# A decoder trunk on one core: more gate and up pairs by seven products, the queries' row earlier, and an end by halves of the tokens

## The chip, the cores and the metric

The kernel runs on one core of a Trainium2 chip. Its engines work from queues of their own and wait for one another by semaphores: TensorE (PE, matmuls into PSUM), VectorE (DVE), ScalarE (ACT), GpSimd (POOL) and SyncE (SP, here only for DMA). The metric is the device time of one execution in microseconds (us), as the median of several runs. A profile is one execution, recorded instruction by instruction.

## The reference

Input x is (1, 512, 1024) in float32; width D is 1024, the feed-forward width 2816, there are 16 heads of 64 and two layers. Layer 0 mixes tokens by a convolution, layer 1 by stick-breaking attention against keys and values that are projected once between the layers:

```python
h = x
for layer in range(2):
    h = h + 0.5 * swiglu_ffn(rms_norm(h, ffn1_norm[layer]), ...)
    u = rms_norm(h, mix_norm[layer])
    if layer < 1:
        h = h + conformer_conv(u, ...)
    else:
        q = split_heads(u @ attn_w_q[0])
        o = stick_breaking_attention(q, k_shared, v_shared)
        h = h + o.transpose(0, 2, 1, 3).reshape(b, s, d) @ attn_w_o[0]
    h = h + 0.5 * swiglu_ffn(rms_norm(h, ffn2_norm[layer]), ...)
    if layer == 0:
        k_shared, v_shared = ...   # rms_norm(h, kv_norm) @ w_kv, in heads
return rms_norm(h, final_norm)

def swiglu_ffn(x, w_gate, w_up, w_down):
    return (silu(x @ w_gate) * (x @ w_up)) @ w_down
```

There are four feed-forward blocks. They are called stages 0 to 3 here, as the kernel numbers them.

## The kernel before

Everything is kept transposed: a tile has 128 channels as partitions and the 512 tokens as columns, and the residual stream `res` is eight such tiles. Every float32 operand of a matmul is split into a high and a low part (`hi` by a cast on ACT, `lo` by a subtraction on DVE, function `split`), and `mm3` makes three matmuls of each product: hi·hi, hi·lo, lo·hi. Weights arrive as units of 128 × 1024 by DMA on SP into `raw` (three buffers) and are split into `whi` and `wlo` (three buffers each). `unit()` takes the oldest unit and fetches another one ahead, in the order that `weight_order` lists. All tiles come from pools: a tile with a tag and `bufs=n` takes the place of the n-th tile before it and waits until that one is no longer read.

A feed-forward block (`ffn`) goes through 22 tiles f of the hidden width in thirds of 8, 8 and 6. For each f, a pair of products gives gate and up (`pg`); then SiLU, a product and a split give `hhi`, `hlo`. After each third come the eight down products (`pd`), each added to `res`. The norm's factor for each token (`rb`, the row `r`) is multiplied in behind the products; `Norm.factor` makes it: squares are summed over chunks (`acc`), over channels by matmuls with a column (`token_sums`, `ss`), then a root in small steps on DVE (`inv_root`), diagonal tiles (`dg`) of the roots' two parts, and matmuls with ones which spread these over all partitions (`spread`, `pb`).

A pair can be made in a second way, listed in the table `SEVEN` by stage. Gate and up weights and two chunks of x are seen as 2 × 2 blocks, and a scheme of seven products takes the place of eight, on quarters: a weight tile of 128 columns against half of the tokens (256). `sevens` prepares the left-hand sums (`st`, split into `sh`, `sl`; `uh`, `ul`), `right_sums` the right-hand ones, once in a stage behind each of the pairs 0 to 3 (`ts`, split into `thi`, `tlo`). `seven` makes 7 products of 4 × 3 matmuls, 84 of 256 columns, where the direct way has 48 of 512. In the profile the direct ones stand under L389 to L391 (`pg<-`), the quarters under L551 to L553.

In attention, `project_values` and `project_keys` (which also makes the queries `pq`) fill PE between the heads' work; `PROJECTIONS` says which projection stands behind which pair of heads. Their outputs share two PSUM banks (`pj`). `project_keys` calls `n_mix.factor` once, in its first run, and keeps the row in `rq`; each `pq` is multiplied by it into `qt`.

The program is written in order, and a scheduler with a cost model of its own then orders each engine's instructions; `tc.manual_schedule` keeps the written order. The convolution has a planner, which the change does not touch. At the end, the last norm's row is made behind the last down product, and eight results are written out, six by DVE and two by ACT and POOL.

## Time and profile before

| | us |
|---|---|
| median of 3 runs | 1923.2 (1921.57 to 1923.63) |
| profiled execution, its own time | 1922.7 |
| its span, from the first to the last instruction | 1920.9 |
| mean granted clock of PE | 0.995 of full |

The span is what the trace covers; 1.8 us lie around it. By the trace, stage 0 goes from the start to about 343 us, the convolution to about 559, stage 1 to about 884, stage 2 to about 1265, attention to about 1549 and stage 3 to 1904; the rest is the last norm and the output. Rows of the trace show start (us), duration (us), engine, line, operation, output and inputs by the program's names without their numbers, partitions and sizes, and in brackets the engine's idle time before it with what ended it. Matmuls overlap in the pipeline: their durations are longer than the spacing of their starts.

### The profile page before, as it was taken

What the parts mean: (1) busy time and instruction counts of PE and PEld (TensorE: products, weight loads), DVE (VectorE), ACT (ScalarE), POOL (GpSimd) and SP (SyncE); (2) the same over time, 40 slices, a digit from 0 to 9 for tenths busy, and PEclk for the clock granted to TensorE, in tenths of its full rate; (3) what the DMA queues carried; (4) which work ended last, traced back from release to release, by engine and by line L of the source; (5) the groups of instructions that cost most, each with busy time, mean ns of one, the idle gap of its engine ahead of it and who ended that gap; (6) DMA issues with size and microseconds to landing.
All of it is one profiled execution on the core that took longest, in us unless ns stands there. A gap on an engine that the chain in (4) does not pass through costs nothing.

```text
span 1920.9 us, 25824 instructions
## 1 busy us (share of the span) xinstructions
PE 1892.0 (98%) x9996; PEld 1621.6 (84%) x9996; DVE 1281.6 (67%) x2054; ACT 862.5 (45%) x1347; POOL 276.3 (14%) x261
## 2 busy tenths in 40 slices
PE   9999999999999999999999999999999999999997
PEld 7888888878998889898888988888888788888895
DVE  6544534598868567466875756768999768466575
ACT  5424323686544234244332433546778544233332
POOL 0302202089600000000000000004543100000000
PEclk9999999999999999999999999999999999999998
DMA  5756746444422333233333333442232223323322
GB/s 201 254 180 239 267 145 229 155 162 151 138 88 88 110 95 103 90 96 112 121 110 109 100 99 92 127 150 77 84 88 89 65 89 99 95 92 99 110 85 69
DMA packets 72522, 237.79 MB, mean 124 GB/s; under 512 B 8272, under 2 KB 8400, under 8 KB 72400
## 3 DMA queue, kind: packets, MB, share of 16 engines
q1 hardware_dynamic: 64624, 209.40, 34.2%
q10 hardware_dynamic: 7776, 26.74, 3.7%
q8 instruction: 78, 1.28, 0.3%
q14 instruction: 44, 0.36, 0.1%
HBM read 200.46 MB, written 31.46 MB: 121 GB/s over the span
## 4 chain that ended last, share of the span: by engine, by line
PE 93%; DVE 3%; ACT 2%; POOL 1%; DMA 1%; issue 1%; DVEq 0%; POOLq 0%; ACTq 0%
PE pg L389 11%; PE pg L391 11%; PE pg L390 11%; PE pd L389 8%; PE pd L390 8%; PE pd L391 8%; PE pg L553 5%; PE pg L552 5%; PE pg L551 5%; PE z L1187 2%; PE pa L389 1%; PE pa L391 1%; PE pa L390 1%; POOL ws L869 1%; PE po L389 1%; PE pv L389 1%
## 5 line engine op out<-in xcount | busy, mean ns | idle before, releaser
L244 ACT CAST whi<-raw 128x1024 fp32r<-128x1024 f32 (+2 forms) x306 | 312.1, 1026 | 612.9 <-PE pd L390 232.1
L245 DVE TENSOR_TENSOR wlo<-raw,whi 128x1024 fp32r<-128x1024 f32 (+2 forms) x306 | 371.2, 1217 | 48.7 <-ACT whi L244 48.6
L389 PE MATMUL pg<-xhi_f,whi 128*128 128x512 f32 x976 | 379.7, 391 | 1.3 <-ACT whi L244 1.2
L391 PE MATMUL pg<-xhi_f,wlo 128*128 128x512 f32 x976 | 380.3, 390 | 0.5 <-DVE wlo L245 0.5
L390 PE MATMUL pg<-xlo_f,whi 128*128 128x512 f32 x976 | 380.4, 390 | 0.0
L390 PE MATMUL pd<-hlo,whi 128*128 128x512 f32 x704 | 274.0, 389 | 0.0
L389 PE MATMUL pd<-hhi,whi 128*128 128x512 f32 x704 | 273.0, 391 | 0.5 <-ACT whi L244 0.4
L391 PE MATMUL pd<-hhi,wlo 128*128 128x512 f32 x704 | 271.7, 389 | 0.0
L389 PEld LDWEIGHTS pg<-xhi_f,whi 128*128 128x128 f32 x976 | 183.5, 188 | 39.7 <-ACT whi L244 1.6
L391 PEld LDWEIGHTS pg<-xhi_f,wlo 128*128 128x128 f32 x976 | 183.3, 188 | 38.6 <-DVE wlo L245 1.3
L390 PEld LDWEIGHTS pg<-xlo_f,whi 128*128 128x128 f32 x976 | 183.5, 188 | 36.5
L627 DVE SCALAR_TENSOR_TENSOR xpar<-pd,xpar 128x512 f32<-128x512 f32 x96 | 65.3, 689 | 166.4 <-PE pd L391 166.4
L389 PEld LDWEIGHTS pd<-hhi,whi 128*128 128x128 f32 x704 | 132.2, 188 | 31.5 <-ACT whi L244 5.2
L391 PEld LDWEIGHTS pd<-hhi,wlo 128*128 128x128 f32 x704 | 132.2, 188 | 27.5 <-DVE wlo L245 0.3
L390 PEld LDWEIGHTS pd<-hlo,whi 128*128 128x128 f32 x704 | 132.2, 188 | 26.3
L607 DVE TENSOR_TENSOR tu<-pg,r_f 128x512 f32<-128x512 f32 x61 | 42.1, 690 | 95.6 <-PE pg L391 95.3
L1086 POOL TENSOR_SCALAR_AFFINE_SELECT tri<-ones 128x128 f32<-128x128 f32 x1 | 0.3, 294 | 714.4 <-DVE tu L582 714.4
L869 POOL TENSOR_TENSOR ws<-ws,pr 128x256 f32<-128x256 f32 (+1 forms) x90 | 90.7, 1019 | 58.2 <-ACT pr L867 54.6
L245 POOL TENSOR_TENSOR plo<-praw,phi 128x1024 fp32r<-128x1024 f32 x24 | 58.1, 2422 | 275.9 <-ACT phi L244 269.7
L605 DVE TENSOR_TENSOR tg<-pg,r_f 128x512 f32<-128x512 f32 x61 | 42.0, 690 | 82.6 <-PE pg L391 82.6
L244 ACT CAST hhi<-tu 128x512 fp32r<-128x512 f32 x88 | 54.7, 623 | 91.4 <-DVE tu L582 55.7
L880 DVE SCALAR_TENSOR_TENSOR pc<-gl,xpar,pc 128x512 f32<-128x512 f32 (+1 forms) x145 | 88.4, 647 | 4.1 <-PE pc L859 2.3
(341 smaller groups left out, 3907.2 us busy)
## 6 DMA issues: line engine op xcount, KB each, us to landing
raw<-in_gu_dram SPq DMA_DIRECT2D x174, 512.0 KB, 3.6
raw<-in_dna_dram SPq DMA_DIRECT2D x64, 512.0 KB, 3.6
praw<-in_pw_dram SPq DMA_DIRECT2D x24, 512.0 KB, 4.2
aparth<-phi ACTq DMA_DIRECT2D x24, 512.0 KB, 2.6
apartl<-plo ACTq DMA_DIRECT2D x24, 512.0 KB, 3.9
raw<-in_dnb_dram SPq DMA_DIRECT2D x32, 384.0 KB, 3.1
whi<-aparth SPq DMA_DIRECT2D x21, 512.0 KB, 3.3
wlo<-apartl SPq DMA_DIRECT2D x21, 512.0 KB, 4.2
```

What stands on the lines that cost most here:

```text
L244: ins = A.copy(dst_hi, src)
L245: (G if on_pool else V).tensor_sub(dst_lo, src, dst_hi.bitcast(F32))
L389: PE.matmul(ps, w[0], x[0], start=first, stop=False)
L390: PE.matmul(ps, w[0], x[1], start=False, stop=False)
L391: PE.matmul(ps, w[1], x[0], start=False, stop=last)
L551: PE.matmul(d, a[0], b[0], start=first and q == 0, stop=False, skip_group_check=True)
L552: PE.matmul(d, a[0], b[1], start=False, stop=False, skip_group_check=True)
L553: PE.matmul(d, a[1], b[0], start=False, stop=last_, skip_group_check=True)
L607: V.tensor_mul(tu, pt[1], rb)
L627: V.scalar_tensor_tensor(res[d], pd, 0.5, res[d], op0=ALU.mult, op1=ALU.add)
L869: add("G", 1.28 * f + 0.1 * half, lambda pr=pr: G.tensor_add(accp, accp, pr()[:, at0]), r=[pr], w=[at_], rank=rank)
L880: add("V", 0.66 * f + 0.06 * half, lambda x=x, q=q: V.scalar_tensor_tensor(pc(), x(), q, pc(), op0=ALU.mult, op1=ALU.add), r=[gl], w=[pc], ...
```

## The change

There are four edits.

1. `SEVEN` lists 11, 10 and 11 pairs in stages 1, 2 and 3, where it listed 9 in each. Some follow directly on one another, and the last pair of each third is a direct one.
2. For room, two buffers become single: `st` (with `ts`), and the parts of a seven-product pair's second weight unit, which leave the three buffers of `whi` and `wlo` for one of their own.
3. The queries' row is made at attention's head, ahead of all projections.
4. The last three down products of stage 3 and the last norm go by halves of the tokens, in an order written by hand (`tail`). The first half's row is made beside the second half's products. DVE reads one PSUM copy of the row, ACT another. The list of `parts` in `Norm`, used at the end alone, goes.

```diff
-SEVEN = {1: (5, 7, 9, 11, 13, 15, 17, 19, 21), 2: (5, 7, 9, 11, 13, 15, 17, 19, 21), 3: (5, 7, 9, 11, 13, 15, 17, 19, 21)}
+STS = 1
+SEVEN = {1: (5, 6, 8, 9, 11, 12, 14, 16, 17, 19, 20), 2: (6, 8, 10, 11, 13, 14, 16, 17, 19, 20), 3: (5, 6, 8, 9, 11, 12, 14, 16, 17, 19, 20)}
...
         hi, lo = (
-            [wp.tile([P, UNIT], F32R, name=f"{n}{i}_{o}", tag=n, bufs=3) for o in range(2)]
+            [wp.tile([P, UNIT], F32R, name=f"{n}{i}_0", tag=n, bufs=3),
+             p.tile([P, UNIT], F32R, name=f"{n}{i}_1", tag=n, bufs=1)]
             for n in ("whi", "wlo")
         )
...
-        st = p.tile([P, UNIT], F32, name=f"st{i}", tag="st", bufs=2)
+        st = p.tile([P, UNIT], F32, name=f"st{i}", tag="st", bufs=STS)
...
-                t = hp.tile([P, 2 * T], F32, name=f"ts{idx}_{q}", tag="st", bufs=2)
+                t = hp.tile([P, 2 * T], F32, name=f"ts{idx}_{q}", tag="st", bufs=STS)
...
-                for d in range(NC):
+                for d in range(NC - TAIL if tail is not None and third == 2 else NC):
...
-            rq = []
+            rq = n_mix.factor(ps, ("z", "z"), bufs=Z_BANKS)
+            V.tensor_scalar_mul(rq, rq, HD ** -0.5)
...
-                if not rq:
-                    rq.append(n_mix.factor(ps, ("z", "z"), bufs=Z_BANKS))
-                    V.tensor_scalar_mul(rq[0], rq[0], HD ** -0.5)
...
+        a, b, e = ds                      # down products 5, 6, 7; second argument: half of the tokens
+        with tc.manual_schedule(engines={nc.tensor.engine, nc.vector.engine, nc.scalar.engine, nc.gpsimd.engine}):
+            product(a, 0)
+            leave(a, 0)                   # add to res on DVE, square on ACT
+            add(a, 0)                     # add to acc on DVE
...
+            product(e, 0)
+            leave(e, 0)
+            product(a, 1)
+            sums(0)                       # token sums on PE
+            product(b, 1)
+            leave(a, 1)
+            for d in (3, 4, 5):
+                gain(d, 0)                # ACT's part of a result
+            root(0)                       # DVE
+            product(e, 1)
+            leave(b, 1)
+            diagonal_rows(0)              # one half each on DVE and ACT
+            row(0)                        # PE, two copies
+            add(a, 1)
+            leave(e, 1)
+            add(b, 1)
+            sums(1)
+            rows(0)                       # copy of the row on ACT
+            for d in (6, 7):
+                gain(d, 0)
+            for d in (0, 3, 1, 4, 2, 5, 6, 7):
+                scale(d, 0)               # POOL for those with a gain, else DVE; DMA out
+            for d in (5, 6, 7):
+                gain(d, 1)
+            root(1)
+            diagonal_rows(1)
+            row(1)
+            rows(1)
+            for d in (0, 5, 1, 2, 6, 3, 4, 7):
+                scale(d, 1)
```

What the scheduler makes of it is seen at three places. First PE in stage 1, within the pairs 5 and 6, which are the first two seven-product pairs in a row; a name like `pg1_6_0` is stage, pair and accumulator. Before, behind four products of pair 5, direct matmuls of pair 6 follow:

```order
L552 MATMUL pg1_5_0_5600<-xlo_f2_0_7_4902,whi99_0_5427 128x256
L553 MATMUL pg1_5_0_5600<-xhi_f2_0_7_4901,wlo99_0_5429 128x256
L389 MATMUL pg1_6_0_5707<-xhi_f2_0_1_4889,whi100_5504 128x512
L390 MATMUL pg1_6_0_5707<-xlo_f2_0_1_4890,whi100_5504 128x512
L391 MATMUL pg1_6_0_5707<-xhi_f2_0_1_4889,wlo100_5505 128x512
L389 MATMUL pg1_6_0_5707<-xhi_f2_0_2_4894,whi100_5504 128x512
L390 MATMUL pg1_6_0_5707<-xlo_f2_0_2_4895,whi100_5504 128x512
L551 MATMUL pg1_5_1_5601<-thi1_0_1_5209,whi99_1_5428 128x256
```

Now pair 6 is in quarters, and behind its first ones stand direct matmuls of pair 7:

```order
L553 MATMUL pg1_5_1_5601<-thi1_3_1_5495,wlo99_1_5430 128x256
L551 MATMUL pg1_6_1_5716<-thi1_0_0_5207,sh100_5517 128x256
L552 MATMUL pg1_6_1_5716<-tlo1_0_0_5208,sh100_5517 128x256
L551 MATMUL pg1_6_2_5717<-thi1_0_0_5207,sh100_5517 128x256
L552 MATMUL pg1_6_2_5717<-tlo1_0_0_5208,sh100_5517 128x256
L393 MATMUL pg1_7_0_5822<-xhi_f2_0_1_4889,whi101_5553 128x512
L394 MATMUL pg1_7_0_5822<-xlo_f2_0_1_4890,whi101_5553 128x512
L395 MATMUL pg1_7_0_5822<-xhi_f2_0_1_4889,wlo101_5554 128x512
```

So between a pair's quarters and those of the next, work of a third pair has been moved in. Second, ACT at attention's head (`vs` are values, `ks` keys, `r_mix` is the queries' row). Before, the row's copy stands behind the casts of three weight units and the first keys:

```order
L1125 CAST vs1_11269<-pv0_3_11357 128x2x64
L244 CAST whi212_11387<-raw212_11386 128x1024
L1138 CAST ks0_0_11417<-pk0_11392 64x512
L1138 CAST ks0_1_11418<-pk0_11392 64x512
L244 CAST whi213_11427<-raw213_11426 128x1024
L244 CAST whi214_11691<-raw214_11690 128x1024
L414 COPY r_mix_1_11477<-pb_mix_1_11481 128x512
L1138 CAST ks1_0_11721<-pk1_11696 64x512
```

Now it stands between the last two copies of values:

```order
L247 CAST whi207_11482<-raw207_11481 128x1024
L247 CAST whi208_11488<-raw208_11487 128x1024
L1129 CAST vs0_11493<-pv0_3_11582 128x2x64
L418 COPY r_mix_1_11461<-pb_mix_1_11465 128x512
L1129 CAST vs1_11494<-pv0_3_11582 128x2x64
L247 CAST whi209_11612<-raw209_11611 128x1024
L1142 CAST ks0_0_11642<-pk0_11617 64x512
```

Its place has moved ahead of the first keys. Third, ACT's queue at the end. Before:

```order
L469 ACTIVATE sq_out_7_17265<-xpar_69 128x512
L1287 ACTIVATE out7_17324<-xpar_69 128x512
L1282 COPY rs_17315<-pb_out_17302 128x512
L1291 DMA out_0_dram<-out0_17321 128x512
L1291 DMA out_0_dram<-out6_17317 128x512
L1291 DMA out_0_dram<-out2_17331 128x512
L1291 DMA out_0_dram<-out4_17337 128x512
```

Now, from the copy of the first half's row on (`out6` and `out4` wait for POOL):

```order
L1360 COPY rs_out0_17696<-pb_out0a_17683 128x256
L1345 ACTIVATE out6_17698<-xpar_69 128x256
L1345 ACTIVATE out7_17700<-xpar_69 128x256
L1356 DMA out_0_dram<-out0_17702 128x256
L1356 DMA out_0_dram<-out4_17630 128x256
L1356 DMA out_0_dram<-out2_17712 128x256
L1356 DMA out_0_dram<-out6_17698 128x256
L1345 ACTIVATE out5_17632<-xpar_69 128x256
L1345 ACTIVATE out6_17698<-xpar_69 128x256
L1345 ACTIVATE out7_17700<-xpar_69 128x256
L1332 ACTIVATE dg_out1_0_17742<-ident_76,dp_out1_17739 128x128
L1332 ACTIVATE dg_out1_1_17745<-ident_76,dp_out1_17739 128x128
```

The diagonals of the second half's row, which the results of that half need, stand behind four DMAs and three gains.

More of the change, by code (lines that the diff above doesn't have):

```diff
@@ L64 @@
 PR_BUFS = 3
+TAIL = 3
 WARM = 10
@@ L422, in token_sums, with inv_root @@
                           start=i + b == 0, stop=i == len(src) - 1, skip_group_check=True)
-    def inv_root(y, v, name):
-        t = tp.tile([P, v.shape[-1]], F32, name=f"rt_{name}", tag="rt", bufs=1)
+    def inv_root(y, v, name, p=None):
+        t = (p or tp).tile([P, v.shape[-1]], F32, name=f"rt_{name}", tag="rt", bufs=1)
         V.tensor_scalar(y.bitcast(I32), v.bitcast(I32), 1, None, op0=ALU.logical_shift_right)
@@ L438, in decoder_kernel, with __init__ @@
     class Norm:
-        def __init__(self, name, gain, pool=None, apart=False):
+        def __init__(self, name, gain, pool=None):
             self.name, self.gain, self.pool = name, gain, pool or xp
@@ L446, in __init__ @@
             self.n = 0
-            self.parts, self.apart = [self.acc], apart
             self.order = []
@@ L469, in square @@
                 A.activation(sq, res[c], AF.Square)
-                if self.apart and self.n == NC - 1:
-                    self.parts.append(sq)
-                else:
-                    V.tensor_add(self.acc, self.acc, sq)
+                V.tensor_add(self.acc, self.acc, sq)
             self.n += 1
@@ L477, in factor @@
             ss = ps.tile([P, 4], F32, name=f"ss_{self.name}", tag=tags[0], bufs=bufs)
-            token_sums(ss, *self.parts)
+            token_sums(ss, self.acc)
             small = tp.tile([P, 4], F32, name=f"rs_{self.name}", tag="rs", bufs=1)
@@ L484, in factor, with ffn @@
             return spread(ps, small, self.name, r, tag=tags[1], bufs=bufs)
-    def ffn(idx, norm, done, early=None, beside=None, sums=None, late=None):
+    def ffn(idx, norm, done, early=None, beside=None, sums=None, late=None, tail=None):
         with ExitStack() as c:
@@ L634, in ffn @@
                             beside(pp_)
+            if tail is not None:
+                tail(c, ps, hid, hp)
     with ExitStack() as c:
@@ L763, in decoder_kernel @@
         add("-", 5.0, lambda: None, w=["acc"])
-        add("PE", 0.7, lambda: token_sums(ssm(), *n_mix.parts), r=["acc"], w=[ssm], rank=-2)
+        add("PE", 0.7, lambda: token_sums(ssm(), n_mix.acc), r=["acc"], w=[ssm], rank=-2)
         add("V", 8.0, mix_diagonals, r=[ssm], w=["dgm"], rank=-2)
@@ L1295, in _lay @@
+    ffn(3, n_f2, n_out.chunk, tail=tail)
 def _lay(a):
```

86 lines of the change are left out of this document (70 added, 16 removed).

## The prediction

> **What bounds the kernel now.** I read the page first: busy shares, the chain that ended last, the waits of PE. Then time in windows, and single instructions where PE waits or changes shape.
>
> ```profile
> span 1920.9 us, 25824 instructions
> PE 1892.0 (98%) x9996; PEld 1621.6 (84%) x9996; DVE 1281.6 (67%) x2054; ACT 862.5 (45%) x1347; POOL 276.3 (14%) x261
> PE 93%; DVE 3%; ACT 2%; POOL 1%; DMA 1%; issue 1%; DVEq 0%; POOLq 0%; ACTq 0%
> ```
>
> TensorE (PE) is busy for 1892.0 of 1920.9 us and carries 93% of the chain that ended last. A change shortens the program if it takes time from PE's stream, or from the few places where PE stands still:
>
> ```profile
> PE pq L389 <- DVE qt L1149: 3.1, 1, 3.1
> PE pg L391 <- DVE wlo L245: 0.5, 1, 0.5
> PE pg L553 <- DVE sl L245: 0.4, 1, 0.4
> ...
> 1276.00:1312.00 36.00, 32.86 (x146) 26.47 (x145) 18.72 (x32) 15.88 (x27) 0.53 (x2) 0.95 0.41 117
> 1312.00:1400.00 88.00, 88.00 (x531) 77.14 (x530) 83.64 (x139) 64.92 (x125) 46.80 (x47) 1.00 0.25 70
> 1480.00:1515.00 35.00, 29.02 (x146) 21.63 (x146) 28.78 (x52) 27.17 (x54) 7.21 (x7) 0.96 0.08 23
> 1297.00:1300.00 3.00, 3.00 (x8) 2.31 (x8) 2.36 (x4) 1.56 (x3) 0.00 (x0) 0.55 0.80 251
> ```
>
> The waits are: line, releaser, total us, times, longest. The windows show stretch, its length, then busy us of PE, weight loads, VectorE (DVE), ScalarE (ACT), GpSimd (POOL), and PE's granted clock. PE lacks about 3 us at attention's head (1276 to 1312) and 6 us at attention's end (1480 to 1515); the program's last 17 us are taken up under D. Between, it is full, and so in attention is DVE: 83.64 of 88 us.
>
> **A: five more pairs by seven products.** A table makes 32 of the 66 pairs of stages 1 to 3 by seven products, where 27 were. Matmuls overlap, so their cost is the spacing of starts:
>
> ```profile
> 589.65 0.39 PE L391 MATMUL pg<-xhi_f,wlo 128*128 128x512 f32 x1
> ...
> 608.01 0.39 PE L391 MATMUL pg<-xhi_f,wlo 128*128 128x512 f32 x1
> 608.24 0.28 PE L551 MATMUL pg<-xhi_f,whi 128*128 128x256 f32 x1
> ...
> 613.87 0.28 PE L553 MATMUL pg<-xhi_f,wlo 128*128 128x256 f32 x1
> ```
>
> From 589.65 to 608.01 there are 81 spacings of 512 columns: 0.2267 us each. From 608.24 to 613.87 there are 47 of 256: 0.1198. A direct pair has 48 of the first, 10.88 us; a seven-product pair 84 of the second, 10.06. The difference of 0.82, five times, is −4.1 us. Nothing hides this, because PE is the bound. The Trainium skill (TensorE: Matmul & The Clock Gate, Back-to-back issue gap) gives a warm spacing of N/2.4 + 2.5 ns, so 215.8 and 109.2 ns. By that the five pairs would save 5.9 us; the trace's spacings are 11 ns longer in both shapes, and the trace decides.
>
> **B: what the pairs in a row may cost.** A seven-product pair loads DVE more:
>
> ```profile
> 615.78 1.22 DVE L245 TENSOR_TENSOR wlo<-raw,whi 128x1024 fp32r<-128x1024 f32 x1
> 616.92 0.68 DVE L337 TENSOR_TENSOR raw<-raw,raw 128x512 f32<-128x512 f32 x1
> 617.52 0.68 DVE L338 TENSOR_TENSOR st<-st,raw 128x512 f32<-128x512 f32 x1
> 618.12 0.42 DVE L562 TENSOR_TENSOR v<-pg,m 128x256 f32<-128x256 f32 x1
> 618.45 0.42 DVE L564 TENSOR_TENSOR tg<-pg,v 128x256 f32<-128x256 f32 x1
> ```
>
> Starts here are 1.14 us apart behind a 1024-wide operation, 0.60 behind 512, 0.33 behind 256. A seven-product pair has on DVE three of 1024 (two `wlo`, `sl`), eight of 512 (four sums, `ul`, two multiplies and `hlo` on the way out) and seven of 256: 3.42 + 4.80 + 2.31 = 10.5 us, against PE's 10.06. A direct pair has 2 × 1.14 + 4 × 0.60 = 4.7 against 10.88. Two in a row and a direct one make 25.7 us for DVE and 31.0 for PE, so DVE keeps up if it can work ahead. Within a row it falls back by 2 × 0.45 = 0.9 us at most if nothing was prepared before. There are 14 such rows (5, 4 and 5 by stage), so the bounds are 0 and +12.6 us.
>
> Two buffers shrink to one as well: the sums (`st`, also the right-hand sums), and the second operand's parts (`whi`, `wlo` of `o` = 1). At the first row (pairs 5 and 6 of stage 1) I followed the queues with these spacings. The last right-hand sums now wait for pair 5's `sl`. They come near 611.1, and PE, which in the new order does 41 quarter matmuls before it reads them, needs them at 608.24 + 41 × 0.12 = 613.2. Pair 6's `sl` comes near 618.5, while PE has 21 direct matmuls of pair 7 in front of it, until about 623. Pair 6's `whi` and `wlo` of `o` = 1 need some 4 us after pair 5's last product, and PE has 28 quarter and 15 direct matmuls, 6.8 us, ahead of them. So margins are 2 to 5 us. The nearest measured row is the pair of short waits above: 0.5 and 0.4 us in all 27 seven-product pairs. I take +1.0 us for the changed rows. That no third ends in seven products I cost at nothing: PE has the down products' matmuls on the earlier `hid` tiles as cover, and without it a pair's way into `hid` (three to four DVE steps of 0.6) would stand open at most 2 us in nine places, as it could before.
>
> **C: the queries' row.** What held PE at attention's head:
>
> ```profile
> 1287.79 0.88 DVE L410 TENSOR_SCALAR dg_mix<-ident,dp_mix 128x128 fp32r<-128x128 f32 x4 [1.45 <-PE pb_mix L411]
> 1293.33 1.05 ACT L244 CAST whi<-raw 128x1024 fp32r<-128x1024 f32 x1 [4.91 <-PE pk L390]
> 1294.40 0.59 ACT L414 COPY r_mix<-pb_mix 128x512 f32<-128x512 f32 x1
> 1296.01 0.69 DVE L1149 TENSOR_TENSOR qt<-pq,r_mix 128x512 f32<-128x512 f32 x1
> 1293.32 0.39 PE L391 MATMUL pk<-kvh,wlo 128*128 128x512 f32 x1
> 1296.84 0.47 PE L389 MATMUL pq<-xhi_mix,whi 128*128 128x512 f32 x1 [3.14 <-DVE qt L1149]
> ...
> 1304.02 0.39 PE L389 MATMUL pk<-kvh,whi 128*128 128x512 f32 x1
> ```
>
> The second query projection needs the bank that `qt` frees. `qt` needs the row, whose copy on ACT stands behind a cast that waits for PE's key projection; half of the diagonals are made only at 1287.79. PE's start to start is 3.52 instead of 0.23, so 3.29 us are lost. Then the clock is 0.55 from 1297 to 1300 and the 24 matmuls take 1304.02 − 1296.84 = 7.18 instead of 5.44: 1.74 more. Sum 5.0. The new order makes all diagonals before the first keys and puts the copy on ACT behind the last values, two projections of 24 matmuls (10.9 us) ahead of the first `qt`. DVE's fourteen small steps of the root (2.7 us by the rows under D) and eight diagonals (2 × 0.88 by the row at 1287.79) run beside two value projections of 24 × 0.12 = 2.9 us each, and ACT's copy beside the first keys. I take −5.0; if a short wait stays the clock may still fall, and only 3.3 us or less are won.
>
> There is more: heads now start after 10 of the second query's 24 matmuls, where they waited for all of them and for 8 of the next keys. That is 22 × 0.227 = 5.0 us earlier in PE's own work. While PE and DVE are both full (1312 to 1400) it earns nothing; it can only fill the 6 us of PE's idle time at attention's end, where DVE has 28.78 of 35. Bounds 0 and −5, and I take −1.0, because DVE still is nearly full there.
>
> **D: the end by token halves.**
>
> ```profile
> 1903.38 0.39 PE L391 MATMUL pd<-hhi,wlo 128*128 128x512 f32 x1
> 1903.61 0.94 PE L421 MATMUL ss_out<-onesD,acc_out 128*128 128x1 f32 x8
> 1903.81 0.69 DVE L627 SCALAR_TENSOR_TENSOR xpar<-pd,xpar 128x512 f32<-128x512 f32 x1 [1.94 <-PE pd L391]
> 1906.36 0.16 DVE L481 TENSOR_SCALAR v_out<-ss_out 128x4 f32<-128x4 f32 x1 [1.87 <-PE ss_out L421]
> 1908.94 0.16 DVE L401 TENSOR_TENSOR dp_out<-rs_out,dp_out 128x4 fp32r<-128x4 f32 x1
> 1911.56 0.59 ACT L1282 COPY rs<-pb_out 128x512 f32<-128x512 f32 x1 [5.73 <-PE pb_out L411]
> 1912.18 4.04 DVE L1290 SCALAR_TENSOR_TENSOR out<-xpar,pb_out 128x512 f32<-128x512 f32 x6 [1.50 <-ACT rs L1282]
> ...
> L869 POOL TENSOR_TENSOR ws<-ws,pr 128x256 f32<-128x256 f32 x45 | 32.7, 739 | 1.9
> L867 ACT ACTIVATE pr<-gl,xpar 128x256 f32<-128x256 f32 x45 | 22.5, 510 | 15.4 <-POOL ws L869 15.3
> ```
>
> Before, the last product starts at 1903.38 and the span ends 17.5 us behind it, of which 4.7 lie behind the last result (1916.22). Ahead of that point PE gets more: 108 × 0.1198 − 54 × 0.2267 = +0.7, and the first half's token sums, about 0.95 (they stand between two products now). Behind the last product, by the same steps at half size: sums read at 2.4 (2.98 before; eviction and square are 0.3 shorter each), root and parts at 5.15. Now ACT must make half of the diagonals, and in its queue three gains of the second half stand behind a DMA that waits for POOL's fourth product of the first half: the first row's copy ends near 1.55, four products and the issue add 4 × 0.74 + 0.3, so 4.8; gains 3 × 0.51 to 6.3, two diagonals of 0.4 to 7.1. PE's row and a copy of half of 0.59 to 8.2, POOL's three to 10.4, and 4.7 to the end: 15.1. That is 2.4 less behind the last product and 1.65 more ahead of it: −0.8 us, if nothing else holds a step. But DVE and POOL hold each other:
>
> ```profile
> 1480.76 0.43 DVE L1201 CAST sh<-a 128x512 fp32r<-128x512 f32 x1
> 1487.93 1.00 POOL L1202 TENSOR_TENSOR sl<-a,sh 128x384 fp32r<-128x384 f32 x1 [2.99 <-PE av L1238]
> 1488.39 0.82 DVE L1201 CAST sh<-a 128x512 fp32r<-128x512 f32 x1
> 1491.95 1.07 POOL L1232 TENSOR_TENSOR wl<-w,wh 128x384 fp32r<-128x384 f32 x1 [3.03 <-PE z L1187]
> 1492.25 1.32 DVE L1202 TENSOR_TENSOR sl<-a,sh 128x512 fp32r<-128x512 f32 x1
> ```
>
> A cast on DVE takes 0.43 us alone and 0.82 when it starts within a POOL operation, ending 0.28 behind it; a subtraction of two SBUF tiles takes 1.32 there, and ends 0.55 behind. In the new end the second half's root (small steps of that kind) runs while POOL makes its five products of the first half, 5 × 0.74 = 3.7 us from 1.55 on. If the root stands until these are done at 5.25, it ends at 8.0 and the diagonals at 8.8 instead of 7.1: +0.9 for the end. If steps slip in between POOL's operations, it is in the middle of −0.8 and +0.9, and I take 0.0. If neither POOL nor ACT's queue held anything, it would be −1.9, the other bound. Eight more DMAs of half the size go out earlier, on queues that have nothing else then.
>
> **Sum.** −4.1 + 1.0 − 5.0 − 1.0 + 0.0 = −9.1. The profiled execution took 1922.7 us (span 1920.9 and 1.8 around it), 0.5 below the median of 1923.2. So 1913.6 by that execution and 1914.1 as a median. Stage 0 and the convolution keep their order: nothing there.
>
> **Rivals.** *The end costs time*: every step of the root waits for POOL, +0.9 as above: 1915.0. The Trainium skill (SBUF — State Buffer, Who interferes with whom) makes this the rule: DVE and POOL share a port pair as an exclusive lock, held for a whole instruction, by DVE operations with two SBUF inputs too. The rows above agree, 0.82 for 0.43 and 1.32 for about 0.68; whether steps of two elements pay as much no run shows yet. Chance 0.17.
>
> *DVE is late in each row*: half of the 0.9 us above, 14 times, is +6.3 instead of +1.0: 1919.4. For it speaks that the buffers are single; against it the 0.9 us in 27 pairs. Chance 0.10.
>
> *The row doesn't do what it says*: the wait moves to the first keys, because PE meets the row's diagonals earlier too: 1914.1 + 5.0 = 1919.1. Chance 0.06.
>
> *Slower*: the single `whi`/`wlo` of the second operand. If PE had nothing between the pairs of a row, the cast (1.05) and the subtraction (1.23) would stand open behind each first pair: 14 × 2.3 = 32 us, 1945 in all. It decides from (9.1 + 1.0)/14 = 0.72 us a row. The new order puts 6.8 us of products there. Chance 0.04.
>
> **Numbers.** My forecast, 1909 to 1918 with the end's two bounds and B's small waits, has 0.60; a larger gain (attention's end filled, below 1909) 0.03. The range, 1909 to 1919, takes in the first rival and leaves out 0.2: that gain, the slower case and most of the late rows and the unmoved wait. A measurement here tells 0.2%, 3.8 us, from no change, so faster needs less than 1919.4: all cases but the slower one and half of the late rows, with a little off for chance: 0.89; same 0.07; slower 0.04.
>
> **What would show it.** Right: 2688 quarter matmuls of pairs at 0.12 us spacing; no wait of `pq` for `qt`, clock 1.00 throughout attention's head; waits of `pg` for DVE or ACT together under 2 us; 16 us from the last product to the end. Wrong: `pg` waits of 0.3 us and more in every row, a clock below 1 in stages 1 to 3, a new wait at the row's matmuls or at attention's end, or root steps at the end more than 0.2 us apart.

## The result, and the profile after

The kernel after takes 1911.2 us (median of 6 runs, 1909.8 to 1911.7) against 1923.2 for the kernel before (6 runs on the same chip): a ratio of 0.9939, with a 95% interval of 0.9929 to 0.9950. The profiled execution has a span of 1909.3 us, 11.6 less than before. The forecast was 1914.1. The size is near, but the parts of the sum are not, as the rest shows.

The page of after, first its head and busy shares, then the shares of the chain that ended last:

```profile
span 1909.3 us, 26551 instructions
...
PE 1885.5 (99%) x10234; PEld 1631.0 (85%) x10236; DVE 1318.3 (69%) x2131; ACT 871.6 (46%) x1381; POOL 287.0 (15%) x267
...
PE 93%; DVE 2%; ACT 2%; POOL 1%; issue 1%; DMA 0%; POOLq 0%; DVEq 0%; ACTq 0%
```

PE is busy for 6.5 us less than before; the other 5.1 us of the shorter span are time in which it stood idle. Its waits of after (line, releaser, total us, times, longest):

```profile
PE pb_out1v L1341 <- ACT dg_out L1332: 4.9, 1, 4.9
PE av L1246 <- ACT low L1245: 2.5, 3, 1.2
PE po L393 <- ACT oh L247: 1.3, 1, 1.3
...
PE pv L393 <- ACT whi L247: 0.9, 1, 0.9
...
PE z L1188 <- POOL sl L1226: 0.6, 1, 0.6
...
PE pq L393 <- DVE vs L1130: 0.3, 1, 0.3
PE z L1188 <- POOL sl L1203: 0.2, 1, 0.2
```

The wait of `pq` for `qt` (3.1 us) is gone. New are 0.9 us at the first values (`pv`), which now wait for their weights' cast, and the last three lines, small waits in the middle of attention. Attention in windows (length, then busy us of PE, weight loads, DVE, ACT, POOL, and the clock):

```profile
1272.00:1300.00 28.00, 28.00 (x129) 23.07 (x129) 15.63 (x23) 14.60 (x25) 2.24 (x3) 1.00 0.45 130
1300.00:1475.00 175.00, 173.50 (x992) 147.16 (x990) 164.37 (x270) 130.43 (x249) 89.29 (x84) 1.00 0.28 84
1475.00:1508.00 33.00, 27.82 (x137) 21.19 (x136) 23.73 (x42) 22.51 (x43) 6.57 (x6) 0.92 0.09 24
```

The head of attention is full, at a clock of 1.00. But from 1300 to 1475 us PE now lacks 1.5 us, where it lacked almost nothing (0.04 between 1312 and 1480), and the last stretch lacks 5.2 us, as it lacked 6.0.

To see where time went, I worked out for each stage what PE lost: from each matmul's start to the next one's, less the spacing of its shape (0.2267 us for 512 columns, 0.1198 for 256, and for the rest the shortest usual one). The stretches go from start to start of marked matmuls: attention from stage 2's last down product to the last output projection, the end from the last down product to the span's end. In before, the last down products of stages 0 to 3 start at 367.8, 906.6, 1263.8 and 1903.4 us and the convolution's last product at 552.2; the round bounds given ahead of the prediction are up to 25 us off for stage 0, the convolution and stage 1. All in us, the columns but the last each from one profiled execution:

| kernel | lost in stage 1 | lost in stage 2 | attention, whole | lost in stage 3 | end, whole | median of runs |
|---|---|---|---|---|---|---|
| before | 1.37 | 4.16 | 283.97 | 2.52 | 17.5 | 1923.2 |
| after | 0.66 | 0.62 | 283.87 | 0.67 | 14.0 | 1911.2 |
| row_only | 1.39 | 4.82 | 282.08 | 1.38 | 17.5 | 1920.3 |
| no_row | 0.66 | 0.63 | 288.36 | 1.80 | 14.0 | 1918.3 |
| tail_only | 1.38 | 3.91 | 282.28 | 2.54 | 14.0 | 1920.9 |
| ends_moved | 3.84 | 10.53 | 288.58 | 3.82 | 17.5 | 1937.4 |
| ends_bufs_row | 0.61 | 6.44 | 281.76 | 0.61 | 17.5 | 1921.8 |
| s2_five | 0.66 | 6.46 | 284.73 | 0.67 | 14.0 | 1915.6 |
| third_last | 1.76 | 3.17 | 283.11 | 1.75 | 14.0 | 1914.7 |
| order_x | 0.66 | 1.36 | 284.14 | 1.79 | 14.0 | 1912.3 |
| end_port | 0.66 | 0.62 | 284.82 | 0.67 | 13.5 | 1910.7 |
| light_dve | 0.66 | 0.62 | 277.48 | 0.67 | 14.1 | 1904.0 (one run) |
| wh_act | 0.66 | 0.63 | 281.27 | 0.67 | 13.5 | 1908.5 |

The trace of ends_bufs_row is that of ends_bufs_row2, the same kernel. The medians come from several sessions, in which before took 1922.4 to 1923.2; the ratios below are each to the before of the same session. From before to after, PE's own work falls by 1.64, 0.82 and 1.64 us in stages 1 to 3, and grows by 1.70 at the end of stage 3 for the halves. Lost time falls by 0.71, 3.54 and 1.85; the end is 3.46 shorter, attention 0.10, and stage 0 and the convolution, which run the same instructions, are 0.45 longer. That is −11.6 in all.

### The profile page after: what moved, and what is told of

Same layout as the page of the kernel before. It is cut to its first block, busy times and chain, and to the rows that moved or that the text cites. A ratio compares the mean times of both kernels' runs of the same rounds, so it can differ in the third digit from the quotient of the medians.

```text
span 1909.3 us, 26551 instructions
## 1 busy us (share of the span) xinstructions
PE 1885.5 (99%) x10234; PEld 1631.0 (85%) x10236; DVE 1318.3 (69%) x2131; ACT 871.6 (46%) x1381; POOL 287.0 (15%) x267
## 4 chain that ended last, share of the span: by engine, by line
PE 93%; DVE 2%; ACT 2%; POOL 1%; issue 1%; DMA 0%; POOLq 0%; DVEq 0%; ACTq 0%
PE pg L393 10%; PE pg L395 10%; PE pg L394 10%; PE pd L393 8%; PE pd L394 8%; PE pd L395 8%; PE pg L553 6%; PE pg L552 6%; PE pg L551 6%; PE z L1188 1%; PE pa L393 1%; PE pa L395 1%; PE pa L394 1%; PE po L393 1%; PE po L394 1%
## 5 line engine op out<-in xcount | busy, mean ns | idle before, releaser
L395 PE MATMUL pg<-xhi_f,wlo 128*128 128x512 f32 x896 | 349.2, 390 | 0.6 <-DVE wlo L248 0.5
L393 PE MATMUL pg<-xhi_f,whi 128*128 128x512 f32 x896 | 348.3, 390 | 1.1 <-ACT whi L247 1.1
L394 PE MATMUL pg<-xlo_f,whi 128*128 128x512 f32 x896 | 349.1, 390 | 0.0
L394 PE MATMUL pd<-hlo,whi 128*128 128x512 f32 x686 | 266.2, 389 | 0.0
L395 PE MATMUL pd<-hhi,wlo 128*128 128x512 f32 x686 | 265.1, 389 | 0.0
L393 PE MATMUL pd<-hhi,whi 128*128 128x512 f32 x686 | 264.1, 389 | 0.0
L395 PEld LDWEIGHTS pg<-xhi_f,wlo 128*128 128x128 f32 x896 | 168.3, 188 | 35.7 <-DVE wlo L248 1.4
L393 PEld LDWEIGHTS pg<-xhi_f,whi 128*128 128x128 f32 x896 | 168.4, 188 | 35.3 <-ACT whi L247 2.0
L394 PEld LDWEIGHTS pg<-xlo_f,whi 128*128 128x128 f32 x896 | 168.4, 188 | 33.6
L552 PE MATMUL pg<-tlo,whi 128*128 128x256 f32 x256 | 72.4, 283 | 0.0
```

The source lines that it names most:

```text
L393: PE.matmul(ps, w[0], x[0], start=first, stop=False)
L394: PE.matmul(ps, w[0], x[1], start=False, stop=False)
L395: PE.matmul(ps, w[1], x[0], start=False, stop=last)
L552: PE.matmul(d, a[0], b[1], start=False, stop=False, skip_group_check=True)
```

## The experiments

**The row alone, on before.** In `row_only` edit 3 is the only change. It begins with:

```diff
-            rq = []
+            rq = n_mix.factor(ps, ("z", "z"), bufs=Z_BANKS)
+            V.tensor_scalar_mul(rq, rq, HD ** -0.5)
...
```

> The kernel before with the queries' row at attention's head, and nothing else. By the prediction's step C it takes 6.0 us less than before (1923.2), so 1917.2, and the stretch from stage 2's last down product to the last output projection (283.97 us before) becomes 278. The rival, formed from the two traces: behind its head, attention goes at the pace of the heads' chain over VectorE, ScalarE and GpSimd, and what PE no longer waits for at the head it waits for later. Then the stall of 3.3 us at the second queries is gone and the clock stays at 1.00 there, but the stretch stays within 1 us of 283.97, and the time is 1922 to 1923, plus or minus what a measurement can tell.

Measured: 1920.3, ratio 0.9987 (0.9979 to 0.9996). Attention took 282.08. The stretch of 5.0 us that PE lost at attention's head is gone, but attention is only 1.9 shorter. In `tail_only` below, where PE's order in attention is that of before, it took 282.28, so even these 1.9 are within what such traces differ from one another. Stage 3 loses 1.14 less, because the wait of 1.04 us at its first product, for its weights' cast, went with the new order. Step C's −6.0 does not stand in these surroundings: by the interval the row is worth 0.8 to 4.0 us. That is between the two theories and nearer to the rival, whose stretch "within 1 us of 283.97" the 282.08 misses as well.

**After without the row.** `no_row` is the reverse of that edit, on after.

> The kernel after, with the queries' row made where it was before. By step C it loses 6.0 us against after (1911.2): 1917. By the rival (attention gives back what its head gains) it stays within 1 us of after: 1910.5 to 1912.5, and has the old stall of 3.3 us with a clock near 0.55 behind it, with fewer small waits behind that.

Measured: 1918.3, ratio 0.9973 (0.9963 to 0.9983). By the two ratios the row is worth 0.0034 × 1923 = 6.5 us. So here step C seems to be confirmed, but neither theory holds in both places: alone the row gives 2.5, here 6.5. Attention took 288.36, longer than in before, with the same stall and the same work:

```profile
1289.85 0.47 PE L393 MATMUL pq<-xhi_mix,whi 128*128 128x512 f32 x1 [3.13 <-DVE qt L1152]
```

A comparison of PE's order in attention explains it. The scheduler makes three of them: before and tail_only have one (X), no_row and ends_moved another (Y), row_only, after and the rest a third (Z); wh_act and light_dve have orders of their own. In Y attention took 288.4 and 288.6, in X 282.3 to 284.1, in Z 281.8 to 284.8. So the new table, which stands for stages 1 to 3, had changed the order of attention as well, and the row edit changed it again. Kernels with one and the same order differ by up to 3 us there, which no run explains, so smaller differences between single traces of attention say little.

**One number that changes attention.** `order_x` is no_row with the last seven-product pair of stage 2 moved from 20 to 21. That brings back X.

```diff
-2: (6, 8, 10, 11, 13, 14, 16, 17, 19, 20)
+2: (6, 8, 10, 11, 13, 14, 16, 17, 19, 21)
```

> The kernel no_row (after without the queries' row at attention's head) with one number of stage 2's table changed, 20 to 21. With it the scheduler gives PE in attention the order that before has; no_row, and ends_moved too, have another one, and in both attention took 288.4 to 288.6 us from stage 2's last down product to the last output projection, where before took 284.0. Theory: these 4.5 us are the order's, not the table's. Then attention takes 282 to 284 here, stage 2 0.7 more than in no_row, and the time is 1914 to 1915. Rival: they come from the pairs in a row or from the single buffers, through what is late when attention begins. Then attention takes 288 here too, and the time is 1918 to 1919.

Measured: 1912.3, ratio 0.9946 (0.9931 to 0.9961), even less than the theory said. Attention in windows, of no_row and then of order_x:

```profile
1256.83:1545.19 288.36, 278.21 (x1506) 232.68 (x1506) 234.04 (x399) 186.52 (x345) 94.50 (x92) 0.99 0.27 83
```

```profile
1257.84:1541.98 284.14, 274.99 (x1507) 232.66 (x1506) 235.45 (x399) 186.28 (x345) 90.67 (x92) 0.99 0.27 84
```

Same counts, same work on DVE and ACT, 4.2 us apart. The stall at the queries is in both, and its row in order_x is that of before:

```profile
1290.87 0.47 PE L393 MATMUL pq<-xhi_mix,whi 128*128 128x512 f32 x1 [3.14 <-DVE qt L1152]
```

So a kernel with that stall is only 1.1 us slower than after, which doesn't have it. By the traces it loses 0.7 more in stage 2, whose last third ends in seven products again, 1.1 more at stage 3's first wait and 0.3 more in attention. The row edit removes a stall of 5 us and earns about 1; that it looked like 6 beside no_row is the scheduler's order Y, which the table had brought in and the row edit took out. Why Y is slower I did not settle. No run moves the row with PE's order unchanged, so what the row alone is worth, without any change of order, stays open.

**The end alone.** `tail_only` is before with edit 4 (the table, buffers and row as before).

> The kernel before with only the end by halves of the tokens. By step D no change, 1923.2 (0.0 for the end, between -1.9 and +0.9). By the accounts of the two traces, 1.85 us less (17.5 us behind the last product become 14.05, and PE gets 1.65 more ahead of it): 1921.3. The trace should show 14 us from the start of the last product to the span's end, and four steps of the second half's root on VectorE of 0.55 to 0.65 us, where 0.16 is usual, beside GpSimd's five products.

Measured: 1920.9, ratio 0.9992 (0.9983 to 1.0001). The times alone don't tell it from no change. By the trace, the end is 14.0 instead of 17.5, and PE's own work in stage 3 1.70 more, as accounted; 1.7 more of the span's difference lie in attention, whose order on PE is that of before.

**Thirds that don't end in seven products, with the old buffers.** `ends_moved`:

```diff
-SEVEN = {1: (5, 7, 9, 11, 13, 15, 17, 19, 21), ...
+SEVEN = {1: (5, 6, 9, 11, 13, 14, 17, 19, 20), ...
```

> The kernel before with another table: nine seven-product pairs in each stage as before, so the same matmuls, but none is the last of a third, and three times two follow on one another (5, 6, 9, 11, 13, 14, 17, 19, 20). By step B the ends of thirds cost nothing and rows cost 0.07 each: 1923.2 to 1924. By the rival from the traces, waits behind a seven-product pair that ends a third are what before loses at 886, 1012, 1243 and 1883 us, 0.7 + 1.3 + 0.7 + 0.7 us of PE: they go, rows cost nothing, and the time is 3.4 less, 1919.8. The wait of 1.3 us near 965 us (pair 5 of stage 2) should stay in either case, since that pair stays the first.

Measured: 1937.4, ratio 1.0072 (1.0058 to 1.0086): a loss of 14 us that neither theory had. The waits at the thirds' ends are gone, but nearly each row of two is followed by a new one. PE in stage 1, the direct pair behind pairs 5 and 6, and that wait's sum over the program:

```profile
622.76 0.28 PE L553 MATMUL pg<-thi,sl 128*128 128x256 f32 x1
623.93 0.50 PE L389 MATMUL pg<-xhi_f,whi 128*128 128x512 f32 x1 [0.90 <-ACT whi L244]
```

```profile
PE pg L389 <- ACT whi L244: 7.6, 9, 1.2
```

Of these nine, seven stand behind a row (0.90 and six of 0.78, 5.6 us in all); the other two are at the program's start and at stage 3's first product. Each of the seven costs PE 0.94 to 1.06 us from start to start. Pairs 5 and 6 of stage 3 have no such wait. In stage 2, where the pairs 5 and 6 follow the right-hand sums, 7.8 us are lost between 967 and 984 us, where before loses 1.35 at pair 5; 2.8 of them behind the waits, at a granted clock of 0.50 from 977.7 to 983.6. Attention has order Y, 4.6 us more.

**The buffers.** `ends_bufs_row` adds edit 2 to this, and the row for order Z.

```diff
-            [wp.tile([P, UNIT], F32R, name=f"{n}{i}_{o}", tag=n, bufs=3) for o in range(2)]
+            [wp.tile([P, UNIT], F32R, name=f"{n}{i}_0", tag=n, bufs=3),
+             p.tile([P, UNIT], F32R, name=f"{n}{i}_1", tag=n, bufs=1)]
...
```

> The kernel before with three of the four edits, but no less work for PE: the table of the kernel ends_moved (nine pairs in each stage, three rows of two, none last in a third), the buffers of edit 2, and the row of edit 3, with which PE's order in attention is that of the kernel after. To compare with ends_moved, whose rows cost 0.94 to 1.06 us each, each time as one wait of the direct pair behind the row for the cast of its weights (whi). First theory: that wait comes from the shared ring of three buffers, of which a row's four units take all, and with a buffer of its own for each second unit it goes; the waits at the thirds' ends stay away too. Then stage 1 loses 0.7 us of PE's time (1.37 before, 3.84 in ends_moved), stage 3 0.7 to 0.9, and only the wait near 965 us remains in stage 2 (1.3 to 5.2). The time is 1916 to 1920. Rival: rows wait because ScalarE and VectorE come late in them, whatever the buffers; then stages 1 and 3 lose 3.5 us each as in ends_moved, and the time is 1926 or more.

> The same kernel as ends_bufs_row, whose profiled execution fell in a disturbed stretch of the chip (a clock of 0.74), for its trace. Its time was 1921.8. By the theory that the buffers make rows free, stages 1 and 3 lose 0.7 to 0.9 us of PE's time each, and all that the table costs stands near 965 us in stage 2 (3 to 6 us lost, where before lost 4.2). By the rival the rows of stages 1 and 3 still wait near 1 us each.

Measured: 1921.8, ratio 0.9993 (0.9983 to 1.0003). Stages 1 and 3 lose 0.61 each, where ends_moved lost 3.84 and 3.82 (1.1 of the latter at stage 3's first wait, which goes with order Z): with a buffer of its own for the second unit, a row costs nothing, and the thirds' ends cost nothing either. All that is left stands in stage 2, 5.9 us from 964 to 979. The first theory holds in its mechanism; its time was 2 us too low, because stage 2 loses what ends_moved lost there.

**Stage 2's first pair.** `s2_five` gives after's stage 2 the table of stages 1 and 3.

```diff
-2: (6, 8, 10, 11, 13, 14, 16, 17, 19, 20)
+2: (5, 6, 8, 9, 11, 12, 14, 16, 17, 19, 20)
```

> The kernel after with stage 2's table replaced by that of stages 1 and 3: eleven pairs that begin with 5 and 6, where after has ten that begin with 6. By step A it takes 0.8 us less than after (1911.2): 1910.4. By the rival, VectorE has no time for a seven-product pair right behind the right-hand sums of stage 2, where it makes the inputs of keys and values as well: PE waits near 965 to 980 us as in ends_moved, 1.3 to 5.2 us, and the time is 1912 to 1916.

Measured: 1915.6, ratio 0.9963 (0.9949 to 0.9977). Stage 2 loses 5.84 more. Waits of PE there, from 955 to 985 us; after has no wait in the same stretch:

```profile
PE pg L551 <- ACT sh L247: 1.1, 1, 1.1
PE pg L551 <- DVE v L562: 0.8, 1, 0.8
PE pg L551 <- ACT m L556: 0.5, 1, 0.5
```

With these come five waits of 0.2 to 0.4 us. No single releaser stands out: everything that feeds a seven-product pair is late at once. One more such pair saves 0.8 and loses 5.8 where it makes a row right behind the sums; pair 5 without pair 6, as in before, loses 1.35 there.

**Thirds that end in seven products, with the new buffers.** `third_last` has as many such pairs as after:

```diff
-1: (5, 6, 8, 9, 11, 12, 14, 16, 17, 19, 20), 2: (6, 8, 10, 11, 13, 14, 16, 17, 19, 20)
+1: (5, 7, 9, 10, 12, 13, 15, 16, 18, 19, 21), 2: (6, 7, 9, 10, 12, 13, 15, 17, 19, 21)
```

> The kernel after with as many seven-product pairs (11, 10 and 11) and the same buffers, but a seven-product pair at the end of each third (7, 15 and 21 in each stage). PE's order in attention is that of after. By step B a third's end costs nothing: 1911.2. By the traces, the waits of before come back: 0.7 us at the end of each stage's last third, and 1.3 at the end of stage 2's second, 3.4 in all: 1914.6. If the single buffers make it worse, each of the nine ends costs 1 us or more: 1920.

Measured: 1914.7, ratio 0.9958 (0.9943 to 0.9973), as the traces of before had it. PE at the second third's end of stage 2, in before and then here:

```profile
1012.76 0.51 PE L389 MATMUL pd<-hhi,whi 128*128 128x512 f32 x1 [0.21 <-ACT whi L244]
1013.70 0.50 PE L389 MATMUL pd<-hhi,whi 128*128 128x512 f32 x1 [0.21 <-ACT whi L244]
```

```profile
1010.65 0.51 PE L393 MATMUL pd<-hhi,whi 128*128 128x512 f32 x1 [0.21 <-ACT whi L247]
1011.60 0.50 PE L393 MATMUL pd<-hhi,whi 128*128 128x512 f32 x1 [0.22 <-ACT whi L247]
```

The down products get their weights late, not the pair's way into `hid`: by the trace, three casts of weight units on ACT stand together from 1008.60 on, once a down product has ended ACT's wait of 3.54 us, where after has three spread from 1003.81 to 1009.03. Of the 4.7 us that third_last loses more than after in stages 1 to 3, 0.5 stand elsewhere, at 980 us between the pairs 6 and 7 of stage 2.

**The end without GpSimd beside the root.** `end_port` moves results:

```diff
-            for d in (3, 4, 5):
-                gain(d, 0)
+            gain(3, 0)
...
-            for d in (0, 3, 1, 4, 2, 5, 6, 7):
+            for d in (0, 3, 1, 2):
                 scale(d, 0)
...
             root(1)
             diagonal_rows(1)
+            rows(0, row=2)                    # second copy of the first row, on ACT
+            for d in (6, 7):
+                scale(d, 0, nc.sync, row=2)   # POOL
+            for d in (4, 5):
+                scale(d, 0, "later")          # DVE; sent with the second half
...
```

> The kernel after with another order of its last results, so that GpSimd does nothing while VectorE makes the second half's root: of the first half's eight results, VectorE makes three and GpSimd one ahead of the root (GpSimd made five); GpSimd's other two read a second copy of the first row, which stands on ScalarE behind the second half's diagonals, and VectorE makes the last two while PE spreads the second row. Those two chunks (4 and 5) leave in one transfer each for both halves. If the four steps of 0.55 to 0.65 us on VectorE are GpSimd's doing, at most one stays, the root takes 2.8 to 3.3 us from its first step to its last instead of 4.6, and the last result comes 1.5 to 2 us earlier. The transfers then stand closer together on their two queues, so that the time is 0.8 to 1.9 us less than after (1911.2): 1909.3 to 1910.4. If the slow steps have another cause (the sums just read from PSUM, or the first steps of a root as such), they stay and the time is the same or 0.5 more, since two results more come late.

The root of the second half in after (POOL's five products first, then steps on DVE):

```profile
1896.78 3.45 POOL L1350 TENSOR_TENSOR out<-out,rs_out 128x256 f32<-128x256 f32 x5 [396.04 <-DVE out L1353]
```

```profile
1896.24 1.25 DVE L1353 SCALAR_TENSOR_TENSOR out<-xpar,pb_out0v 128x256 f32<-128x256 f32 x3
1897.46 0.16 DVE L1319 TENSOR_SCALAR v_out<-ss_out 128x2 f32<-128x2 f32 x1
1897.66 0.55 DVE L431 TENSOR_SCALAR y_out<-v_out 128x2 int32<-128x2 int32 x1
1898.25 0.65 DVE L432 TENSOR_SCALAR y_out<-y_out 128x2 int32<-128x2 int32 x1
1898.93 0.64 DVE L436 TENSOR_TENSOR rt_out<-y_out 128x2 f32<-128x2 f32 x1
1899.60 0.65 DVE L437 SCALAR_TENSOR_TENSOR rt_out<-v_out,rt_out 128x2 f32<-128x2 f32 x1
1900.28 0.16 DVE L438 SCALAR_TENSOR_TENSOR y_out<-rt_out,y_out 128x2 f32<-128x2 f32 x1
...
1901.85 0.16 DVE L1323 TENSOR_TENSOR dp_out<-y_out,dp_out 128x2 fp32r<-128x2 f32 x1
```

And in end_port:

```profile
1897.70 0.73 POOL L1350 TENSOR_TENSOR out<-out,rs_out 128x256 f32<-128x256 f32 x1 [396.09 <-DVE out L1353]
1901.98 1.42 POOL L1350 TENSOR_TENSOR out<-out,acc_out 128x256 f32<-128x256 f32 x2 [3.56 <-ACT acc_out L1364]
```

```profile
1898.39 0.16 DVE L1319 TENSOR_SCALAR v_out<-ss_out 128x2 f32<-128x2 f32 x1
1898.58 0.17 DVE L431 TENSOR_SCALAR y_out<-v_out 128x2 int32<-128x2 int32 x1
1898.79 0.17 DVE L432 TENSOR_SCALAR y_out<-y_out 128x2 int32<-128x2 int32 x1
...
1900.96 0.16 DVE L1323 TENSOR_TENSOR dp_out<-y_out,dp_out 128x2 fp32r<-128x2 f32 x1
```

With GpSimd out of the way every step takes 0.16 to 0.17, and the root ends 2.57 us behind its first step instead of 4.39. The Trainium skill (SBUF — State Buffer, Who interferes with whom) makes the port pair that the two engines share a lock held for a whole instruction; the trace agrees, down to steps on two elements, each of which stood until one of GpSimd's products was done, while what reads PSUM beside at most one SBUF tile, the three results from 1896.24 on and the step at 1897.46, took its usual 0.42 and 0.16. Two of the four steps that stood (L431 and L432) read one SBUF tile only; by that section such a step is held only in a mode that uses both ports, and no run here shows in which mode they ran. The time is 1910.7, ratio 0.9938 (0.9925 to 0.9952), which the times alone don't tell from after's 0.9939; by the trace the end is 13.47 instead of 14.04. So the cause of the slow steps is shown, but of the 1.8 us saved on the root 0.6 reach the end: the last result comes at 1905.45, 9.3 us behind the last product instead of 10.9, and then 4.2 us instead of 3.1 pass to the span's end, with the transfers now close together.

**Who sets the pace of attention?** `light_dve` is after with less work on VectorE; it leaves out low parts of the attention weights, so its output is not the reference's:

```diff
...
-                    (G if g in WL_POOL else V).tensor_sub(wl, w, wh.bitcast(F32))
+                    if g in WL_POOL:
+                        G.tensor_sub(wl, w, wh.bitcast(F32))
+                    else:
+                        wl = wh
```

> The kernel after, with VectorE's subtractions of the attention weights left out (wl of the groups 0 and 2 of each head; the matmuls take wh in its place, so PE has as many as before, and the output lacks those low parts). This takes some 20 us of work from VectorE in attention. PE's order changes with it. If VectorE sets the pace of attention (95% busy there), which would be why heads that start 14 us earlier gain nothing, attention shrinks by 5 us or more, from 283.9 to 279 or less. If PE sets it until the last projection, and then the chain of the last heads, only the small waits between 1310 and 1460 us (3 us in all) and one or two steps of the chain can go: 281 to 283.

Attention in windows, in after, then in light_dve:

```profile
1257.57:1541.44 283.87, 276.31 (x1505) 232.00 (x1506) 234.90 (x399) 187.02 (x345) 98.10 (x92) 0.99 0.28 85
```

```profile
1256.94:1534.42 277.48, 272.20 (x1506) 231.08 (x1507) 209.97 (x367) 189.31 (x345) 91.38 (x92) 0.99 0.28 87
```

Measured: 1904.0, one run. DVE's work falls by 24.9 us and attention by 6.4, with PE's work the same. PE's lost time falls by 3.8 up to the first output projection and by 2.6 behind it, in the chain of the last heads. 277.48 is also 4.3 below the lowest of the kernels with order Z. So VectorE's steps hold attention back, though PE is busy 97% of it. Whether by their load, or because each head no longer waits for these subtractions, this run can't separate, and part of the 6.4 may be the new order. The 14 us of the expectation were read from the span's start; counted from stage 2's last down product the heads start 8.3 us earlier than in before.

**A version that uses this.** `wh_act` is end_port with 32 casts moved to ACT:

```diff
-                    V.tensor_copy(wh, w)
+                    (V.tensor_copy if g in WL_POOL else A.copy)(wh, w)
```

> The kernel end_port with 32 casts of attention's weights (wh of the groups 0 and 2 of each head) moved from VectorE (0.34 us from start to start for most) to ScalarE (about 0.6). In light_dve, 24.9 us less work on VectorE made attention 6.4 us shorter. If VectorE's load alone is what counts, some 14 us less work give 3.6: attention 280.2 and the time 1907. ScalarE gets 19 us more (187 of 284 us before) and stands in each head's chain ahead of wl, 0.2 us longer for each group; if that chain is what counts, the last heads' wait grows by 1 to 2 us and attention is the same or up to 3 us longer: 1911 to 1914. PE's order in attention changes, which alone was worth up to 4.5 us in the kernels so far.

```profile
1257.04:1538.31 281.27, 274.24 (x1507) 231.31 (x1506) 219.74 (x367) 203.46 (x377) 89.88 (x92) 0.99 0.28 85
```

Measured: 1908.5, ratio 0.9927 (0.9913 to 0.9941). Attention is 3.55 shorter than in end_port, for 16.1 us less on DVE and 16.5 more on ACT, though the cast and the subtraction still stand in each head's chain: that speaks for VectorE's load. The Trainium skill (Perfetto Trace Analysis, Optimizing Scalar/DVE Operations) advises moving work to ScalarE where DVE is saturated; this run goes that way, but 281.27 is only 0.5 below the shortest attention with order Z, PE's order is another one, and the intervals of the two ratios overlap, so the gain is not shown beyond doubt. By its median it is the fastest of these kernels that compute the whole reference.

## Why the prediction was right in size and wrong in its parts

| step | predicted | measured, from before to after |
|---|---|---|
| A, five more seven-product pairs | −4.1 | −4.1 |
| B, table and buffers, beyond that | +1.0 | −5.0 |
| C, row and earlier heads | −6.0 | −1.2 (attention −0.1, stage 3's first wait −1.1) |
| D, the end | 0.0 | −1.76 (+1.70 ahead, −3.46 behind) |
| stages without a change | 0 | +0.45 |
| sum | −9.1 | −11.6 |

**A** held to the tenth: 11, 10 and 11 pairs with spacings of 0.1198 and 0.2267 us, and in the stages of the change nothing lost beyond 0.7 us.

**B** failed at three of its sentences. *That no third ends in seven products I cost at nothing*: the thirds' ends cost before 3.5 us (0.7, 2.1 and 0.7 by stage, from start to start), and with the new buffers some 4.2 in third_last. I looked at the pair's way into `hid` and left out the casts of the down weights, though the waits stood in the trace of before, each under 0.4 us and so small in any list. *Bounds 0 and +12.6*: below nothing was not considered, though before lost 4.16 us in stage 2; 2.1 of these went with the thirds' ends and 1.35 because the first pair of stage 2 is now 6. *Two buffers shrink to one as well*: I took the single buffers for a price. For `whi` and `wlo` the buffer of its own is what makes rows possible; with the shared ring most rows cost 1.0 us, so 14 rows would have cost about 14 by estimate, near the upper bound. The rival "slower", built on that buffer, had the sign of its effect reversed. One reading was wrong as well: of the two waits "in all 27 seven-product pairs" the one of 0.5 us stands at 18.67 us, in stage 0, which has no such pair. After's list has no wait of `pg` in stages 1 to 3 at all; its 1.1 and 0.5 us are at the program's start.

**C** was right about the stall and wrong about its worth. The wait of 3.29 us and the slow clock are gone, as the window from 1272 to 1300 shows. Counted from stage 2's last down product, the heads start 8.3 us earlier (first `sh` product 42.97 us behind it, at 1300.54, for 51.25, at 1315.07), but the last output projection stands at the same distance. The sentence that failed is *sum 5.0*: I took PE's idle time on the chain for time gained, although the same fence showed DVE at 83.64 of 88 us behind it, and I had used this only against the further −1.0. PE gives the time back elsewhere: 1.0 at the first values (0.9 of it idle), for a cast of their weights, and 2.4 in five places between 1319 and 1459 of 0.36 to 0.77 from start to start, for steps of GpSimd and VectorE; the last heads lose nearly as much as before (5.2 for 6.0 us of idle time), and the rest is in smaller pieces. That VectorE is what holds the heads is borne out by light_dve and wh_act, with the reserve made there. The rival for this step had nearly the right price, +5.0, at the wrong place (the first keys). And beside order Y the same edit is worth 6.5, so the term has no single value: it depends on an order that another edit sets.

**D** was too careful, for a cause other than the one weighed. The lock did hold the root: its second to fifth step took 2.6 us for 0.8, so 1.8 more, one step for each of GpSimd's products. That is the middle case of the forecast, not the rival's, in which the root stands until all five are done, 2.85 later. It is also the sign of being wrong that I had named, steps more than 0.2 us apart. ACT's queue, the other worry, did not matter: its gains ended at 1901.28, ahead of the root's last step at 1901.85. But the span ended 3.1 us behind the last result, where I had carried over 4.7 from transfers of twice the size.

That the sum came within 3 us was luck: two errors of opposite sign, 6.0 too little in B and 4.8 too much in C, and 1.8 too little in D.

## What to carry to other kernels

A stall on the critical engine need not be worth its length where another engine is nearly full behind it: before counting it, look at the other engines' shares there. Where a scheduler with its own cost model orders the program, test each edit in both surroundings, and compare the order of stages that it doesn't touch; here one number in one stage moved another stage by 4 us. Add up small waits of the same place over a stage, since five of 0.2 to 0.4 us never show in a list of the longest.

## What I had not expected of the hardware

Steps of VectorE on two elements per partition, 0.16 us alone, took 0.55 to 0.65 beside GpSimd's 256-wide products of 0.69, one step for each product, and ran at 0.16 to 0.17 in end_port. And from the last result to the span's end it took 4.7 us in before (128 × 512 per transfer), 3.1 in after (128 × 256), and 4.2 in end_port, where halves and two whole chunks leave together.
